# A decoder layer in fp32: operands of the second half of the tokens made one by one from sums kept in DRAM, its first weights split a pair ahead, and the zero blocks of attention written by ScalarE

## The chip, the cores and the metric

The kernel runs on one core of a Trainium2 chip. The metric is device time in microseconds (us), given as the median of three runs. All work is float32.

## The reference

One layer of a decoder with S = 2048 tokens, width D = 1024, 16 heads of 64 and an MLP of width 2752; cut to what matters:

```python
mod = silu(c) @ w_ada + b_ada              # shift, scale, gate for the mixer and for the MLP
h = rms_norm(x, g_attn) * (1 + scale_a) + shift_a
q_f, k_f, v_f, q_s, k_s, v_s, f_logit = split(h @ w_in)
o_fox = forgetting_attention(...)          # 8 heads: softmax(qk/8 + F[t] - F[s]), F = cumsum(log f)
o_sb = stick_breaking_attention(...)       # 8 heads: sigmoid(z) * prod of (1 - sigmoid(z)) between
mix = concat(head_rms_norm(o_fox), head_rms_norm(o_sb))
x = x + gate_a * (mix @ w_out)
h = rms_norm(x, g_mlp) * (1 + scale_m) + shift_m
u = causal_depthwise_conv(h @ w_up, conv_w, conv_b)   # w_up: 1024 x (2752 gate + 2752 value), width 3
x = x + gate_m * ((silu(u_gate) * u_val) @ w_down)
return rms_norm(x, g_final)
```

## The kernel before

*Split products.* A float32 factor is split into a high part (ScalarE copies it to the type fp32r) and a low part (VectorE or GpSimd subtracts the high part from it); `split`, lines 43 to 45, does both. A product is then three matmuls: high by high, high by low, low by high.

*Stages.* Projections and attention run first, interleaved unit by unit. In attention, blocks of weights are transposed on TensorE (L388) into a bank `ps_pt`, split into `at` (L392 on ScalarE, L393 on VectorE), and multiplied with V (L397). For a block on the causal diagonal the part of `at` ahead of the block is zero; `weighted` writes it at L391, 128 times in all, on GpSimd, which also multiplies the stick-breaking weights `a` (L420). Then the out-projection runs over eight units of 256 tokens (`mix` is its input, `x1` the residual). `finish_out` (L705) normalises a unit of `x1`, transposes it on TensorE, modulates it into `hf_m` (two buffers, ScalarE) and stores `hf_m` to DRAM (`hms`) from ScalarE's queue.

*Up-projection.* It runs over two halves of 1024 tokens (`sblk` 0 and 1), and in each over 21 pairs of 128 gate columns and 128 value columns, then over a tail of 64 and 64. A pair is a 2x2 by 2x2 block product (gate and value by two halves of D, two halves of D by two runs of 512 tokens), done with seven products for eight. Each product takes one of seven operands of the weights (`wu`, made anew for each pair from sums that GpSimd forms) and one of seven operands of h, numbered 0 to 6 (0, 2, 3 and 5 lie in `oa`, 1, 4 and 6 in `ob`), which serve a whole half. A product is four row blocks j of 128 by three matmuls of 512 columns: 12 matmuls, 84 a pair. The tail uses operands 0, 2, 3 and 5 alone: 48 matmuls.

`h_operands(sblk, j)` makes row j of all seven operands: two loads of 512 KB into `xh` on SyncE's (SP's) queue, four differences on GpSimd and VectorE, and the splits. Row 0 lies in the pool `hop0`, which is open from the out-projection on; rows 1 to 3 lie in `hop1`, opened over the space that the out-projection's pools held. Each row has one buffer, so the second half's row waits until the first half's last product has read it. The first pair of a half (`pair_first`, L821) goes row by row over seven banks:

```python
for j in range(NK):
    for s in (1, 4, 6, 0, 2, 5, 3):
        product(banks[s], ws[s], obs[j][0][s], j, j == 0, j == NK - 1)
```

In the other pairs (`pair`) each product runs whole, and the weight operands of the next pair (`nxt`) are made between its products. The weights of the first pair of each half are made beside `h_operands`.

*Down-projection.* `load` (L926) brings a block of `w_down` (`wdraw`, L935) and of the gated result (`graw`, L936) on SP's queue, and splits both; `xo` (L975) is the residual read back.

*Order.* Each engine and each queue works in order. The order is set by the framework's scheduler, which simulates the program and picks the next instruction for each engine; only dependencies, buffer counts and the order of the code steer it.

Of the kernel before, what the change touches and what calls it, by code (L numbers as in the profile page):

```python
# [16 lines left out]
P = 128  # L17
S = 2048
D = 1024
KT = D // P  # L20
# [13 lines left out]
def kernel(ctx: ExitStack, tc: tile.TileContext, x, c, w_ada, b_ada, g_attn, w_in, b_fgate,  # L34
# [17 lines left out]
    hms = [[dram.tile([P, 2 * TB], F32, name=f"hm{s}_{k}") for k in range(KT)] for s in range(2)]  # L52
# [329 lines left out]
    def weighted(o, kts, blk, V, hl, first, last, diag):  # L382
# [7 lines left out]
        if diag:  # L390
            nc.gpsimd.memset(f(at[:, :, 0:P]), 0.0)  # L391
# [313 lines left out]
    def finish_out(u, xts):  # L705
        sl = slice(u % 4 * HT, (u % 4 + 1) * HT)
# [3 lines left out]
        for kt in range(KT):  # L710
# [3 lines left out]
            hf = p2b.tile([P, HT], F32, name="hf_m", bufs=2)  # L714
            nc.scalar.activation(hf, ps[:, :HT], AF.Identity, scale=mod_m[:, 0, kt:kt + 1],
                                 bias=mod_m[:, 1, kt:kt + 1])
            nc.scalar.dma_start(hms[u // 4][kt][:, sl], hf)
# [21 lines left out]
    NK = KT // 2  # L739
    SB = 2 * TB  # L740
# [9 lines left out]
    def h_operands(sblk, j):  # L750

        pool = ho if j == 0 else ho1
        xh = ho.tile([P, 2, SB], F32, name="xh", bufs=2)
        for i in range(2):
            nc.sync.dma_start(xh[:, i], hms[sblk][j + i * NK])
        b = pool.tile([P, 3, 2, TB], F32R, name=f"ob{j}")
        a = pool.tile([P, 4, 2, TB], F32R, name=f"oa{j}")
        tt = ho.tile([P, 2, TB], F32, name="tt", bufs=1)
        t4 = wp.tile([P, TB], F32, name="t4", tag="ws", bufs=3)
        b11, b12 = xh[:, 0, 0:TB], xh[:, 0, TB:SB]  # L760
        b21, b22 = xh[:, 1, 0:TB], xh[:, 1, TB:SB]

        def put(hi, lo, s, lo_engine=None):
            split(hi, lo, s, lo_engine or nc.vector)

# [42 lines left out]
    def product(b, w, o, j, first, last):  # L808
        for i, (p, q) in enumerate(((0, 0), (0, 1), (1, 0))):
            nc.tensor.matmul(b, w[:, p, j], o[:, q], start=first and i == 0, stop=last and i == 2,  # L810
                             skip_group_check=True)

    def snap():
        return up_.tile([P, TB], F32, name="snap", bufs=4)
# [6 lines left out]
    def pair_first(ws, yg, yv):  # L821
# [3 lines left out]
        for j in range(NK):  # L825
            for s in (1, 4, 6, 0, 2, 5, 3):
# [194 lines left out]
```

## Time and profile before

| | |
|---|---|
| median of 3 runs | 3139.62 us (3137.22 to 3140.04) |
| the profiled execution | 3137.58 us, of it the profile's span 3135.8 |
| busy: TensorE matmuls, weight loads | 2962.9, 2508.4 us |
| busy: VectorE, ScalarE, GpSimd | 2142.5, 1650.2, 1281.3 us |
| DMA | 496.51 MB, mean 158 GB/s |
| projections and attention | to about 1590 us |
| out-projection | to 1776.2 us |
| up, first half, its first pair | to 2207.6 us, 1811.6 us |
| up, second half | to 2644.4 us |
| down | 2653.1 us to the end |

Times are from the span's start. A row of a group gives line, engine, operation, output, inputs, shape, count, then busy time and the mean of one in ns. A row of waits gives who waits, for whom, and us in all, times, longest. A row of the timeline gives start and length of a run of instructions, and in brackets the idle time ahead of it with what ended it. PE is TensorE, PEld its weight load, DVE VectorE, ACT ScalarE, POOL GpSimd, SPq the issuing of DMAs by SyncE.

### The profile page before, as it was taken

The numbers are of one execution on the slowest core, as the hardware profiler recorded it, in microseconds if no ns is written. First come the engines' busy times: TensorE is split into PE (matmuls) and PEld (weight loads), VectorE is DVE, ScalarE is ACT, GpSimd is POOL, SyncE is SP. The second block draws the span as 40 slices with busy tenths as digits, with TensorE's granted clock in tenths as the row PEclk, the third lists the DMA queues.
The fourth block names the chain that finished last, engine by engine and source line by source line (L and its number), as shares of the span: only waits on it lengthen the run. The fifth ranks groups of instructions, "written<-read, shape, count | busy, mean of one in ns | idle before, by whom it ended". The sixth has DMA issues, their size and how long they took to land. (4 is left out here: it accounts for less than half of the span.)

```text
span 3135.8 us, 46430 instructions
## 1 busy us (share of the span) xinstructions
PE 2962.9 (94%) x15934; PEld 2508.4 (80%) x15934; DVE 2142.5 (68%) x3334; ACT 1650.2 (53%) x3033; POOL 1281.3 (41%) x1523
## 2 busy tenths in 40 slices
PE   6889998999989999999999899999899998999998
PEld 5778787878878888888877688888678887888887
DVE  6787988888866765557832677778887776254253
ACT  5665666666656665567733444444444444333332
POOL 2564455456553343352212444444544442332321
PEclk8999999999999999999999999999999999999999
DMA  9447642556346796595456532223222223554552
GB/s 268 170 149 250 175 139 64 189 178 167 124 150 184 258 279 209 152 328 137 161 186 220 195 98 81 81 81 88 77 89 86 81 81 137 186 199 161 188 200 89
DMA packets 292940, 496.51 MB, mean 158 GB/s; under 512 B 29448, under 2 KB 177664, under 8 KB 291680
## 3 DMA queue, kind: packets, MB, share of 16 engines
q1 hardware_dynamic: 281072, 480.92, 48.0%
q10 hardware_dynamic: 11632, 12.63, 1.1%
q8 instruction: 126, 2.06, 0.3%
q14 instruction: 110, 0.90, 0.1%
HBM read 352.61 MB, written 90.51 MB: 141 GB/s over the span
## 5 line engine op out<-in xcount | busy, mean ns | idle before, releaser
L810 PE MATMUL ps_o<-oa,wu 128*128 128x512 f32 x2088 | 506.2, 393 | 18.1 <-DVE oa L45 12.0
L810 PEld LDWEIGHTS ps_o<-oa,wu 128*128 128x128 f32 x2088 | 392.4, 189 | 110.0 <-DVE oa L45 15.7
L397 PE MATMUL ps_pv<-at,V 128*128 128x256 f32 x2304 | 404.7, 294 | 36.2 <-DVE at L393 19.5
L393 DVE TENSOR_TENSOR at<-ps_pt,at 128x512 fp32r<-128x512 f32 (+1 forms) x576 | 364.0, 652 | 107.2 <-ACT at L392 104.2
L281 PE MATMUL ps_pj<-hp,w_qk 128*128 128x512 f32 x1512 | 415.2, 405 | 14.2 <-DMA hp<-hs 4.4
L392 ACT ACTIVATE at<-ps_pt 128x512 fp32r<-128x512 f32 (+1 forms) x576 | 314.4, 576 | 210.2 <-PE ps_pt L388 161.0
L420 POOL TENSOR_TENSOR a<-a,r 128x512 f32<-128x512 f32 (+3 forms) x240 | 286.8, 1196 | 309.8 <-DVE r L419 88.5
L397 PEld LDWEIGHTS ps_pv<-at,V 128*128 128x128 f32 x2304 | 334.6, 191 | 81.0 <-DVE at L393 34.5
L281 PEld LDWEIGHTS ps_pj<-hp,w_qk 128*128 128x128 f32 x1512 | 275.6, 191 | 68.7 <-DMA hp<-hs 6.9
L45 DVE TENSOR_TENSOR wd<-wdraw,wd 128x1024 fp32r<-128x1024 f32 x88 | 111.8, 1271 | 263.0 <-ACT wd L44 262.9
L45 POOL TENSOR_TENSOR g<-graw,g 128x512 fp32r<-128x512 f32 x84 | 142.3, 1696 | 326.5 <-ACT g L44 325.8
L378 PE MATMUL ps_qk<-K,Q 128*128 128x512 f32 (+2 forms) x640 | 265.7, 417 | 9.6 <-DMA K<-q 5.6
L419 DVE TENSOR_TENSOR_SCAN r<-r 128x513 f32<-128x513 f32 x192 | 258.9, 1360 | 19.4 <-ACT r L410 11.5
L960 PE MATMUL ps_o<-wd,g 128*128 128x512 f32 x1040 | 251.1, 391 | 8.7 <-ACT g L44 8.7
L810 PE MATMUL ps_t<-ob,wu 128*128 128x512 f32 x984 | 242.5, 391 | 0.3 <-ACT wu L44 0.3
L379 PE MATMUL ps_qk<-K,Q 128*128 128x512 f32 (+2 forms) x640 | 237.8, 373 | 0.0
L320 PE MATMUL ps_pj<-w_v,hp 128*128 128x256 f32 (+1 forms) x1536 | 230.8, 290 | 6.6 <-DVE q L290 2.9
L960 PEld LDWEIGHTS ps_o<-wd,g 128*128 128x128 f32 x1040 | 196.2, 189 | 50.0 <-ACT g L44 9.2
L44 ACT ACTIVATE wu<-wuraw 128x512 fp32r<-128x512 f32 x214 | 133.1, 626 | 184.2 <-PE ps_o L810 111.8
L320 PEld LDWEIGHTS ps_pj<-w_v,hp 128*128 128x128 f32 x1536 | 210.1, 193 | 16.5 <-DVE q L290 3.8
L810 PEld LDWEIGHTS ps_t<-ob,wu 128*128 128x128 f32 x984 | 185.3, 189 | 39.8 <-ACT wu L44 0.7
L44 ACT ACTIVATE wd<-wdraw 128x1024 fp32r<-128x1024 f32 x88 | 93.1, 1058 | 213.3 <-PE ps_bc L960 197.9
(218 smaller groups left out, 5834.1 us busy)
## 6 DMA issues: line engine op xcount, KB each, us to landing
hp<-hs SPq DMA_DIRECT2D x224, 512.0 KB
wuraw<-in_w_up_dram SPq DMA_DIRECT2D x84, 512.0 KB
wdraw<-in_w_down_dram SPq DMA_DIRECT2D x84, 512.0 KB
Q<-q SPq DMA_DIRECT2D x128, 256.0 KB
g<-u SPq DMA_DIRECT2D x42, 512.0 KB
graw<-g SPq DMA_DIRECT2D x84, 256.0 KB
hs<-hp SPq DMA_DIRECT2D x32, 512.0 KB
K<-q SPq DMA_DIRECT2D x128, 128.0 KB
```

Source lines behind the costliest of these rows:

```text
L45: (lo_engine or nc.gpsimd).tensor_sub(lo, src, f(hi))
L281: nc.tensor.matmul(acc, w[kt][:, a, n], h[:, bb], start=kt == 0 and i == 0, stop=kt == KT - 1 and i == 2)
L320: nc.tensor.matmul(av[:, t * width:(t + 1) * width], hts[kt][:, a, tok], w[1][kt][:, bb, 0:width], start=kt == 0 and m == 0, stop=kt == KT ...
L378: nc.tensor.matmul(b[:, :cw], Q[:, hl, 0, qcols], K[:, hl, :cw], start=True, stop=False)
L379: nc.tensor.matmul(b[:, :cw], Q[:, hl, 1, qcols], K[:, hl, :cw], start=False, stop=True)
L392: nc.scalar.activation(at[:, 0, lo:], b[:, lo:], AF.Copy)
L393: nc.vector.tensor_sub(at[:, 1, lo:], b[:, lo:], f(at[:, 0, lo:]))
L397: nc.tensor.matmul(o[:, 0:2 * P], V[kt // 4][:, kt % 4, hl, :], rhs, start=first and kk == 0 and w == 0, stop=last and kk == 1 and w == 1)
L419: nc.vector.tensor_tensor_scan(rev, rev, rev, 1.0, ALU.mult, ALU.bypass)
L420: (nc.vector if (ch + qi) % 4 == 0 else nc.gpsimd).tensor_mul(a[:, :need], a[:, :need], r[:, 1:need + 1])
L810: nc.tensor.matmul(b, w[:, p, j], o[:, q], start=first and i == 0, stop=last and i == 2, skip_group_check=True)
L960: nc.tensor.matmul(banks[t][n], g[:, a, t * P:(t + 1) * P], w[:, b, n * TB:(n + 1) * TB], start=k == 0 and i == 0, stop=k == NKD - 1 and i ...
```

## The change

The operands of h get one tile for each operand (`ob0` to `ob6`, all four rows in one tile, all in `hop1`) in place of one for each row. The normalised h goes to DRAM as quadrants (`hmo`, by half of D and run of 512 tokens), from four `hf_m` buffers. In the first half `h_rows(j)` makes row j of all seven with one split of 512 columns for each operand and row, 28 in all, every low part on VectorE. During the first half, after every third pair, `h_sums` loads a row of the second half's quadrants, forms the four sums on GpSimd and writes them back to DRAM. For the second half `h_operand(o)` loads one operand (1 MB) and splits it whole; its first pair goes operand by operand in the order 1, 4, 6, 0, 3, 2, 5. The weights of that pair are made during pair 20 of the first half. `wu` gets nine buffers for seven, `snap` three for four. In attention the zero block is a copy of zeros by ScalarE.

```diff
-            nc.gpsimd.memset(f(at[:, :, 0:P]), 0.0)
+            nc.scalar.activation(at[:, :, 0:P], edge[:, 0:2 * P].rearrange("p (a n) -> p a n", n=P), AF.Copy)
...
-            hf = p2b.tile([P, HT], F32, name="hf_m", bufs=2)
+            hf = p2b.tile([P, HT], F32, name="hf_m", bufs=4)
...
-            nc.scalar.dma_start(hms[u // 4][kt][:, sl], hf)
+            nc.scalar.dma_start(quadrants[kt // NK][:, kt % NK, sl], hf)
...
+    def square():
+        return ho.tile([P, 2, SB], F32, name="xh", bufs=2)
+
+    def h_quadrants(sblk, j):
+        x = square()
+        q = [x[:, i, n * TB:(n + 1) * TB] for i in range(2) for n in range(2)]
+        for part, o in zip(q, (0, B12, 2, 5)):
+            nc.sync.dma_start(part, hmo[sblk][o][:, j])
+        return q
+
+    def h_rows(j):
+
+        b11, b12, b21, b22 = h_quadrants(0, j)
...
         nc.gpsimd.tensor_sub(tt[:, 0], b22, b12)
         nc.gpsimd.tensor_sub(b12, b12, b11)
         nc.vector.tensor_sub(tt[:, 1], b22, b12)
         nc.vector.tensor_sub(t4, b21, tt[:, 1])
-        put(b[:, 0:2, 0], b[:, 0:2, 1], tt)
-        put(b[:, 2, 0], b[:, 2, 1], t4)
-        put(a[:, 0, 0], a[:, 0, 1], b11)
-        put(a[:, 1:3, 0], a[:, 1:3, 1], xh[:, 1].rearrange("p (a n) -> p a n", n=TB), nc.gpsimd)
-        put(a[:, 3, 0], a[:, 3, 1], b12)
-        return [a[:, 0], b[:, 1], a[:, 1], a[:, 3], b[:, 0], a[:, 2], b[:, 2]], a
+        for o, x in ((1, tt[:, 1]), (4, tt[:, 0]), (6, t4), (0, b11), (2, b21), (5, b22), (3, b12)):
+            split(obs[o][:, 0, j], obs[o][:, 1, j], x, nc.vector)
+
+    def h_sums():
+
+        for j in range(NK):
+            b11, b12, b21, b22 = h_quadrants(1, j)
+            nc.gpsimd.tensor_sub(b22, b22, b12)
+            nc.gpsimd.tensor_sub(b12, b12, b11)
+            nc.gpsimd.tensor_add(b11, b22, b11)
+            nc.gpsimd.tensor_sub(b21, b21, b11)
+            yield
+            for part, o in ((b22, 4), (b12, 3), (b11, 1), (b21, 6)):
+                nc.sync.dma_start(hmo[1][o][:, j], part)
+
+    def h_tile_of(o):
+        return ho1.tile([P, 2, NK, TB], F32R, name=f"ob{o}")
+
+    def h_operand(o):
+
+        raw = square().rearrange("p a (b n) -> p (a b) n", n=TB)
+        nc.sync.dma_start(raw, hmo[1][o])
+        b = h_tile_of(o)
+        split(b[:, 0], b[:, 1], raw, nc.vector)
+        return b
...
-        w = wp.tile([P, 2, NK, P], F32R, name="wu", bufs=7)
+        w = wp.tile([P, 2, NK, P], F32R, name="wu", bufs=9)
...
-        return up_.tile([P, TB], F32, name="snap", bufs=4)
+        return up_.tile([P, TB], F32, name="snap", bufs=3)
...
+        for j, s in ([(j, s) for j in range(NK) for s in ORDER] if by_row else
+                     [(j, s) for s in ORDER for j in range(NK)]):
+            product(banks[s], ws[s], obs[s], j, j == 0, j == NK - 1)
...
-            obs[j] = h_operands(sblk, j)
-            ws.extend(next(gen) for _ in range(2 if j < 3 else 1))
+        if sblk == 0:
+            for o in ORDER:
+                obs[o] = h_tile_of(o)
+            gen = w_operands(0)
+            ws = []
+            for j in range(NK):
+                h_rows(j)
+                ws.extend(next(gen) for _ in range(2 if j < 3 else 1))
+        else:
+            for o in ORDER:
+                obs[o] = h_operand(o)
+        sums = h_sums() if sblk == 0 else None
...
-            nxt = w_operands(ci + 1) if ci + 1 < NFULL else None
+            nxt = w_operands((ci + 1) % NFULL) if ci + 1 < NFULL or sblk == 0 else None
...
-            nc.sync.dma_start(gs[ci][sblk], ug)
+            stored = nc.sync.dma_start(gs[ci][sblk], ug)
+            if sums is not None and ci % 3 == 2:
+                with tc.issue_after(stored.ins):
+                    next(sums, None)
```

How the change moves instructions is shown at three places. The first is VectorE between the end of the out-projection and the first pair of the up-projection. Before (`x1` are the residual tiles, `ps_o` the out-projection's banks, `oa0` and `ob0` row 0 of the operands, `xh` its source):

```order
L45 TENSOR_TENSOR mix_21428<-o_21422,mix_21428 128x256
L633 TENSOR_TENSOR x1_21431<-ps_o_21459,x1_21431 128x512
L45 TENSOR_TENSOR oa0_21776<-xh_21772,oa0_21776 128x512
L633 TENSOR_TENSOR x1_21486<-ps_o_21488,x1_21486 128x512
L768 TENSOR_TENSOR tt_21777<-xh_21772 128x512
L45 TENSOR_TENSOR oa0_21776<-xh_21772,oa0_21776 128x512
L769 TENSOR_TENSOR t4_21778<-xh_21772,tt_21777 128x512
L45 TENSOR_TENSOR ob0_21775<-tt_21777,ob0_21775 128x2x512
L633 TENSOR_TENSOR x1_21486<-ps_o_21514,x1_21486 128x512
L45 TENSOR_TENSOR ob0_21775<-t4_21778,ob0_21775 128x512
```

The same place after (`ob1`, `ob4` and so on are now whole operands; the tiles `ss_m` hold the sums of squares of the normalisation):

```order
L636 TENSOR_TENSOR x1_21652<-ps_o_21654,x1_21652 128x512
L636 TENSOR_TENSOR x1_21652<-ps_o_21680,x1_21652 128x512
L98 RECIPROCAL ss_m_21707<-ss_m_21707 128x2
L713 TENSOR_SCALAR x1_21597<-x1_21597,ss_m_21707 128x1024
L713 TENSOR_SCALAR x1_21652<-x1_21652,ss_m_21707 128x1024
L45 TENSOR_TENSOR ob1_21772<-tt_21784,ob1_21772 128x512
L45 TENSOR_TENSOR ob4_21773<-tt_21784,ob4_21773 128x512
L45 TENSOR_TENSOR ob6_21774<-t4_21785,ob6_21774 128x512
L45 TENSOR_TENSOR ob0_21775<-xh_21779,ob0_21775 128x512
L45 TENSOR_TENSOR ob2_21777<-xh_21779,ob2_21777 128x512
```

The splits of row 0 stood between the last additions to the residual; now every split of the first half follows the normalisation of the last 256 tokens.

The second place is TensorE at the end of the first half. Before (numbers in 25000 belong to the second half's tiles, `ob0_24983` is its row 0; the others are the first half's):

```order
L810 MATMUL ps_o_24916<-oa3_21867,wu_24912 128x512 x3
L810 MATMUL ps_o_24917<-oa0_21776,wu_24912 128x512 x3
L810 MATMUL ps_o_24917<-oa1_21812,wu_24912 128x512 x3
L810 MATMUL ps_o_24917<-oa2_21840,wu_24912 128x512 x3
L810 MATMUL ps_o_24917<-oa3_21867,wu_24912 128x512 x3
L810 MATMUL ps_o_25098<-ob0_24983,wu_25013 128x512 x3
L810 MATMUL ps_t_25101<-ob0_24983,wu_25065 128x512 x3
```

After (names ending in 21772 to 21778 are the first half's operands, `ob4_25093` and `ob1_25088` the second half's):

```order
L830 MATMUL ps_t_24948<-ob4_21773,wu_24816 128x512 x9
L830 MATMUL ps_o_24896<-ob3_21776,wu_24799 128x512 x12
L830 MATMUL ps_t_25127<-ob4_25093,wu_24961 128x512
L830 MATMUL ps_o_24896<-ob5_21778,wu_24832 128x512 x12
L830 MATMUL ps_t_25127<-ob4_25093,wu_24961 128x512 x11
L830 MATMUL ps_o_25022<-ob0_21775,wu_25015 128x512 x2
L830 MATMUL ps_o_25023<-ob3_21776,wu_25015 128x512 x2
L830 MATMUL ps_o_25124<-ob1_25088,wu_24909 128x512 x9
L830 MATMUL ps_t_24948<-ob6_21774,wu_24848 128x512 x12
```

The second half's first products, of operands 4 and 1, now stand among the first half's last, ahead of the tail.

The third place is SP's queue between the up-projection and the down-projection. Before (`u` holds the gated result, `g21_1` its tail in DRAM):

```order
L952 DMA gm_28155<-gate_m_234 128x1024
L953 DMA gf_28156<-in_g_final_dram 128x1024
L935 DMA wdraw_28168<-in_w_down_dram 128x1024
L936 DMA graw_28169<-g0_0_140 128x512
L935 DMA wdraw_28202<-in_w_down_dram 128x1024
L936 DMA graw_28203<-g1_0_142 128x512
L935 DMA wdraw_28236<-in_w_down_dram 128x1024
L975 DMA xo_28821<-x1s0_192 128x1024
L975 DMA xo_28864<-x1s1_193 128x1024
L975 DMA xo_28907<-x1s2_194 128x1024
L975 DMA xo_28950<-x1s3_195 128x1024
L923 DMA g21_1_183<-u_28141 64x1024
```

After:

```order
L984 DMA gf_28182<-in_g_final_dram 128x1024
L1006 DMA xo_28847<-x1s0_192 128x1024
L1006 DMA xo_28890<-x1s1_193 128x1024
L1006 DMA xo_28933<-x1s2_194 128x1024
L1006 DMA xo_28976<-x1s3_195 128x1024
L954 DMA g21_1_183<-u_28167 64x1024
L966 DMA wdraw_28194<-in_w_down_dram 128x1024
L967 DMA graw_28195<-g0_0_140 128x512
L966 DMA wdraw_28228<-in_w_down_dram 128x1024
```

The first loads of `w_down` stood ahead of the residual's loads and of the store of the tail; now they stand behind both.

More of the change, by code (lines that the diff above doesn't have):

```diff
@@ L51 @@
     os_ = [[dram.tile([P, TB], F32, name=f"os{p}_{t}") for t in range(NTB)] for p in range(NPAIR)]
[L52 removed]
+    NK = KT // 2
+    SB = 2 * TB
+    B12 = 7
+    hmo = [[dram.tile([P, NK, TB], F32, name=f"hm{s}_{o}") for o in range(8)] for s in range(2)]
     gs = [[dram.tile([P if k < NFULL else REST, 2 * TB], F32, name=f"g{k}_{s}") for s in range(2)]
@@ L809, in product @@
         for i, (p, q) in enumerate(((0, 0), (0, 1), (1, 0))):
-            nc.tensor.matmul(b, w[:, p, j], o[:, q], start=first and i == 0, stop=last and i == 2,
+            nc.tensor.matmul(b, w[:, p, j], o[:, q, j], start=first and i == 0, stop=last and i == 2,
                              skip_group_check=True)
     def snap():
-        return up_.tile([P, TB], F32, name="snap", bufs=4)
+        return up_.tile([P, TB], F32, name="snap", bufs=3)
     def y_tile():
@@ L842, in run @@
             for j in range(NK):
-                product(b, ws[s], obs[j][0][s], j, first and j == 0, j == NK - 1)
+                product(b, ws[s], obs[s], j, first and j == 0, j == NK - 1)
             if nxt is not None:
@@ L905 @@
         a, b = bank_a(), bank_a()
-        oa = [obs[j][1] for j in range(NK)]
         for j in range(NK):
-            product(a, w1, oa[j][:, 0], j, j == 0, j == NK - 1)
+            product(a, w1, obs[0], j, j == 0, j == NK - 1)
         p1 = snap()
```

33 lines of the change are left out of this document (8 added, 25 removed).

## The prediction

> **What bounds the kernel now.** I read the page's first part and its slices first, to see which engine is full and where it is not; then a table of stretches around the three change-overs of the second half; then the waits of TensorE in each of them, and the timeline at their edges.
>
> ```profile
> PE 2962.9 (94%) x15934; PEld 2508.4 (80%) x15934; DVE 2142.5 (68%) x3334; ACT 1650.2 (53%) x3033; POOL 1281.3 (41%) x1523
> PE   6889998999989999999999899999899998999998
> ```
>
> TensorE (PE) is the bound: 2962.9 of 3135.8 us. A change that leaves its matmuls alone can only win what it idles or runs slowly. The 8s in slices 23, 29 and 34 are the three change-overs around the halves of the up-projection, the last 8 is the program's end. The stretches, with columns of busy time and count for PE, PEld, DVE, ACT and POOL, then granted clock, DMA share and GB/s:
>
> ```profile
> 1776.20:1811.60 35.40, 27.22 (x106) 19.77 (x105) 28.03 (x25) 20.29 (x35) 23.03 (x13) 0.86 0.43 147
> 1811.60:2207.60 396.00, 394.58 (x1729) 323.25 (x1728) 315.71 (x358) 179.38 (x253) 168.38 (x168) 1.00 0.27 82
> 2200.00:2262.00 62.00, 48.94 (x182) 36.48 (x181) 58.51 (x55) 30.81 (x42) 33.65 (x19) 0.89 0.24 72
> 2641.00:2655.00 14.00, 5.27 (x20) 3.95 (x20) 8.36 (x8) 5.76 (x7) 1.81 (x1) 0.79 0.76 269
> 2180.94 2.88 PE L810 MATMUL ps_t<-ob,wu 128*128 128x512 f32 x12
> 2183.66 5.60 PE L810 MATMUL ps_o<-oa,wu 128*128 128x512 f32 x24
> ```
>
> The last two rows give the pitch of a matmul at full clock: 12 from 2180.94 to 2183.66, 0.227 us each. At the middle change-over, 182 matmuls are worth 41.3 us, so the stretch 2200 to 2262 loses 20.7 us. VectorE (DVE) is busy 58.51 of those 62 us: it makes the operands. Inside the first half (1811.6 to 2207.6) PE idles 1.4 us. The waits of TensorE (us, times, longest) in the out-projection, the middle and the down change-over, and of ScalarE (ACT) in the out-projection:
>
> ```profile
> PE ps_t L713 <- ACT hf_m L715: 8.2, 9, 1.8
> PE ps_o L629 <- ACT mix L44: 2.8, 4, 1.0
> ACT hf_m L715 <- DMA hm<-hf_m: 8.6, 6, 3.8
> ACT mix L44 <- DMA hm<-hf_m: 8.1, 3, 2.7
> PE ps_o L810 <- DVE oa L45: 8.9, 4, 4.2
> PE ps_o L960 <- ACT g L44: 8.7, 1, 8.7
> ```
>
> **The change, part by part.**
>
> *Middle change-over: a gain of 17 us.* Today no product of the second half starts before the row of operands it needs is split, and the rows of `oa` stay occupied until the first half's last product. By the order, the new operands 4 and 1 are used while the first half's tail still runs, and the weights are there. What stays is the splitting on DVE:
>
> ```profile
> L45 DVE TENSOR_TENSOR oa<-xh,oa 128x512 fp32r<-128x512 f32 x8 | 13.3, 1688 | 0.0
> L45 DVE TENSOR_TENSOR ob<-tt,ob 128x1024 fp32r<-128x1024 f32 x4 | 4.9, 1218 | 0.4 <-ACT ob L44 0.4
> L45 POOL TENSOR_TENSOR oa<-xh,oa 128x1024 fp32r<-128x1024 f32 x4 | 13.6, 3411 | 0.0
> L45 DVE TENSOR_TENSOR wu<-wuraw,wu 128x512 fp32r<-128x512 f32 x8 | 5.3, 682 | 0.7 <-ACT wu L44 0.7
> ```
>
> Seven splits of 128x2048 are an estimated 2.3 us each on DVE (twice the 1218 ns of 1024 columns, less a start), 16 us in all, and 2 us each on ACT. A 512-column split costs 682 ns alone and 1688 ns beside GpSimd's (POOL's) 3411 ns splits, which go. An operand feeds 12 matmuls, 2.7 us, so 2.3 us keeps up if DVE has little else. It has: at 315.71 of 396 us it is 80% full, so in the 45 us from the pair before to the end of the first pair some 9 us are free for 16; the deeper weight buffers carry part of the rest. Bounds: the whole 20.7 us goes, or, if DVE binds as now, none. I take 4 us left, near the first end, because the splits now spread over the pair before: 17 gained.
>
> *Out-projection: a gain of 7 us.* Four `hf_m` buffers for two. ACT waited 8.6 and 8.1 us for their stores, in front of `hf_m` and `mix`; PE waited 8.2 and 2.8 us behind those. Bounds 0 and 11.0; I take 7, since the bank waits in the 8.2 also include ACT's own work.
>
> *First change-over: a loss of 6.5 us.* By the order, the 28 splits of 512 columns now all follow the normalisation of the last tokens on DVE, and on ACT the last `hf_m`, where before row 0's stood earlier and products started at once:
>
> ```profile
> 1774.48 1.87 PE L629 MATMUL ps_o<-wo,mix 128*128 128x512 f32 x7
> 1776.18 0.85 PE L810 MATMUL ps_o<-ob,wu 128*128 128x512 f32 x3
> 1811.58 2.88 PE L810 MATMUL ps_o<-oa,wu 128*128 128x512 f32 x12
> 1787.82 1.40 DVE L709 TENSOR_SCALAR x<-x,ss_m 128x1024 f32<-128x1024 f32 x2
> 1780.94 1.04 ACT L93 ACTIVATE junk_m<-x 128x1024 bf16<-128x1024 f32 x1
> 1791.34 1.00 ACT L715 ACTIVATE hf_m<-ps_t,mod_m 128x256 f32<-128x256 f32 x2
> 1794.69 1.00 ACT L715 ACTIVATE hf_m<-ps_t,mod_m 128x256 f32<-128x256 f32 x2
> L766 POOL TENSOR_TENSOR tt<-xh 128x512 f32<-128x512 f32 x3 | 5.0, 1675 | 12.0 <-DVE ob L45 12.0
> ```
>
> Call the end of the out-projection T0 (1776.2); the first pair ends at 1811.6, T0+35.4. After: an add, a square, root, reciprocal and two products, about 4 us (1.04 and 1.40 are the large ones); then four pairs of `hf_m`, 1.0 us each with their issues, 3.35 us apart at 1791.34 and 1794.69 with two buffers; I take 2.1 apart with four, 8.5 us. So the first split stands at T0+12.5. Then 28 splits and 6 sums at 0.64 us (682 ns, starts overlapping a little) are 21.8 us; six POOL differences of 1675 ns each slow one DVE step by 1.0 (1688 less 682), 6 us; the last products 1.6. End at T0+41.9, 6.5 later. Bounds: nothing, if the splits find POOL quiet and `hf_m` runs through, to 28 us, if all 28 cost 1688 ns.
>
> *Sums through DRAM: 0.* Sixteen POOL steps of 1675 ns, 16 loads and 16 stores of 256 KB, 7 loads of 1 MB, SP's queue with them. Cover: DVE has 80 us free in the first half and DMA stands at 0.27. If that cover were gone, 16 DVE steps lose 1.0 us each, 16 us; below nothing, the 1.4 us that PE idles, since two more weight buffers are there. Nearer to zero, as 16 is a fifth of the free 80. One `snap` buffer fewer: covered by the same slack; each is read within a pair.
>
> *Down change-over: a loss of 6 us.* The chain there, and what SP's queue issues:
>
> ```profile
> 2636.75 7.64 PE L810 MATMUL ps_o<-oa,wu 128*128 128x512 f32 x33
> 2653.12 2.07 PE L960 MATMUL ps_o<-wd,g 128*128 128x512 f32 x4 [8.73 <-ACT g L44]
> 2645.30 0.44 SPq L935 DMA_DIRECT2D wdraw<-in_w_down_dram  x1
> 2648.05 3.76 SPq L975 DMA_DIRECT2D xo<-x1s  x4
> 2652.44 0.48 SPq L923 DMA_DIRECT2D g<-u  x1
> 2651.49 1.06 ACT L44 ACTIVATE wd<-wdraw 128x1024 fp32r<-128x1024 f32 x1 [1.26 <-DMA wdraw<-in_w_down_dram]
> ```
>
> The first `wdraw` is issued at 2645.30, lands at 2651.5, and PE goes on at 2653.12. In the new order four `xo` loads and the store of the tail's result (2652.44 now, after its convolution, SiLU and product) stand ahead of it in SP's in-order queue. So it is issued near 2652.9, 7.6 us later; the landing, 6.2 us, may be shorter as the 2 MB of `xo` go first. Bounds 0 (if the tail is stored sooner) and 9; I take 6.
>
> *Zero blocks: 0.* 128 of them move from POOL to ACT:
>
> ```profile
> L391 POOL MEMSET at<- x128: 301/312/318, 51.1 to 1583.8; 128x256 f32 x128
> L44 ACT ACTIVATE mix<-o 128x256 fp32r<-128x256 f32 x56 | 23.1, 416 | 71.4 <-POOL o L614 62.8 <-DMA hm<-hf_m 8.1 <-ACT hf_m L715 0.4
> POOL at L391 <- PE ps_pv L397: 160.4, 54, 18.2
> ACT at L392 <- PE ps_pt L388: 161.0, 153, 5.9
> PE ps_pv L397 <- ACT at L392: 4.8, 6, 1.6
> PE ps_pt L388 <- POOL a L420: 10.8, 14, 1.9
> ```
>
> ACT's nearest row has 416 ns, 53 us for 128: the upper bound, all on the path. POOL waits 160.4 us with a zero block at the head of its queue and the products `a` behind it; PE waited 10.8 us for those: the gain at best. ACT mostly waits for the transposes at this place (161.0 us) and hides the zeros there, while PE waited only 4.8 us on ACT. I take 0 between, and the stage is ordered anew, so it holds most of my uncertainty.
>
> Sum: -17 - 7 + 6.5 + 0 + 6 + 0 = -11.5 us. The profiled execution took 3137.58 us (span 3135.8 and 1.8 around it): 3126.1. The median of the runs shown, 3139.62, is 2.0 higher, so on its scale 3128.
>
> **Two rules beside the rows.** After the 8.73 us of idling, the first four matmuls took 2.07 us, more than twice the 0.227 pitch. The Trainium skill, "TensorE: Matmul & The Clock Gate", section "What's actually happening", says that an idle window of about 3.4 us halves the clock until some 3.4 us of work have passed; the row agrees. It speaks against this change: the new idling after T0 would start the first pair at half clock. By the rule that adds up to 1.7 us, an estimate from the page's window; by the rows nothing, since the splits pace those products, and I keep nothing.
>
> A DVE split took 1688 ns beside POOL's against 682. The skill's "SBUF — State Buffer", section "Who interferes with whom", says that a VectorE step with two SBUF inputs contends with a GpSimd step that reads SBUF, not with one that only writes. The slowing agrees; by the rule the removed zero blocks free no VectorE time, which the sum has as 0 already, and the sixteen sums would each block it whole, an estimated 27 us for my 16, still inside the 80 free.
>
> **The rivals.**
> 1. *DVE keeps the middle bound* (0.16). For it: 58.51 of 62 us busy and 16 us of splits that remain. Against it: POOL's 3411 ns splits are gone and the work starts earlier. Then 4 gained for 17: 1.5 us slower, 3141.
> 2. *The first change-over eats the gain; slower* (0.12). All seven tiles lie where out-projection weights and residual tiles lay. If POOL keeps DVE at 1688 ns for all 28 splits, the loss is 28 for 6.5: 10 us slower, 3150. It decides slower from a loss of 24 us on. Against it: only six POOL differences stand there.
> 3. *ACT becomes the bound in attention* (0.09). If half of the 53 us is on the path: 15 us slower, 3155. For it: 1650.2 us busy grows by 53. Against: the 161.0 us.
> 4. *POOL freed pays as well* (0.13). The 10.8 us of PE waits go: 3117.
>
> **How the numbers follow.** My own forecast has 0.50, about 3121 to 3136 from the bounds near each value taken. A change of less than 0.2%, 6.3 us, can't be told from none here: 3133.3 to 3145.9. Faster: 0.43 of the forecast's 0.50 and rival 4's 0.13, 0.56. Same: 0.07 and rival 1's 0.16, 0.23. Slower: rivals 2 and 3, 0.21. The range 3112 to 3150 reaches to rivals 4, 1 and 2 and leaves out 3 and the far ends.
>
> **What the profile after would show.** Right, if PE runs through the middle with under 6 us of waits, restarts 13 to 16 us after the last up product at the down change-over, and stands still some 12 us after the out-projection before its first product. Wrong, if DVE is full again between the halves with PE waiting on its splits, if the splits after the out-projection average over a microsecond, or if PE's waits in attention move by more than 10 us in sum.

## The result and the profile after

The changed kernel takes 3177.47 us (median of 4 runs, 3171.45 to 3181.12) where the kernel before takes 3139.83 (4 runs): a ratio of 1.0112, 95% interval 1.0099 to 1.0125. It is slower by 1.1%; the forecast was 0.4% faster. The profiled execution has a span of 3173.4 us for 3135.8, 37.6 us more. The page's first part and TensorE's slices:

```profile
PE 2974.2 (94%) x15934; PEld 2515.6 (79%) x15934; DVE 2115.2 (67%) x3329; ACT 1683.9 (53%) x3156; POOL 1196.0 (38%) x1395
PE   6889998989989999999999899999999998999998
```

The 8 of the middle change-over (slice 29) is gone, as meant. The engines' sums hardly differ; the loss is spread. To find it, the up-projection's matmuls were counted over the trace: a stretch that ends with the same number of them has about the same work in both kernels. The stretches run from the out-projection's end to matmul 168 (the first two pairs), from 252 to 1680 (first half), from 1680 to 2064 (middle), from 2064 to 3624 (second half). First the four of before, then the four of after; columns are length, then busy time and count of PE, PEld, DVE, ACT and POOL (the counts take in what straddles an edge, and at the start the last transposes), granted clock, DMA share, GB/s:

```profile
1776.20:1831.00 54.80, 46.40 (x189) 35.33 (x187) 45.93 (x45) 29.74 (x48) 33.08 (x24) 0.91 0.35 114
1850.70:2177.30 326.60, 326.10 (x1431) 267.45 (x1430) 255.38 (x290) 144.43 (x205) 138.04 (x136) 1.00 0.27 83
2177.30:2288.50 111.20, 95.72 (x384) 74.29 (x383) 99.03 (x100) 51.27 (x71) 57.00 (x40) 0.94 0.29 88
2288.50:2646.00 357.50, 355.60 (x1562) 291.97 (x1560) 273.21 (x314) 156.42 (x219) 145.94 (x105) 1.00 0.26 79
...
1782.80:1846.40 63.60, 51.23 (x189) 37.47 (x188) 49.78 (x62) 33.70 (x58) 22.71 (x21) 0.84 0.29 91
1866.00:2219.10 353.10, 334.10 (x1428) 269.47 (x1429) 255.78 (x292) 143.98 (x207) 141.68 (x152) 0.99 0.36 105
2219.10:2315.80 96.70, 90.45 (x386) 73.62 (x386) 78.72 (x84) 50.20 (x60) 38.50 (x29) 0.96 0.44 132
2315.80:2678.00 362.20, 356.09 (x1561) 291.91 (x1559) 258.16 (x312) 152.66 (x216) 121.30 (x105) 1.00 0.26 78
```

The end of attention is marked by its last sums over heads (`headsel`), first in the kernel before, then after:

```profile
1588.94 0.61 PE L485 MATMUL ps_pt<-headsel,sq 128*128 128x2 f32 x4 [1.68 <-POOL sq L480]
1602.05 0.61 PE L488 MATMUL ps_pt<-headsel,sq 128*128 128x2 f32 x4 [1.68 <-POOL sq L483]
```

| stretch | forecast, us | measured, us |
|---|---|---|
| projections and attention (zero blocks) | 0 | +13.1 |
| out-projection (187.3 before, 180.8 after) | -7 | -6.5 |
| first change-over, two pairs | +6.5 | +8.8 |
| first half | 0 | +26.5 |
| middle change-over | -17 | -14.5 |
| second half | 0 | +4.7 |
| down change-over (from matmul 3624 to the restart: 7.1, 14.1) | +6 | +7.0 |
| the rest | 0 | -1.5 |
| sum | -11.5 | +37.6 |

The edges of the rows lie up to 1.7 us beside the matmul that they stand for. Taken at the matmuls themselves, the first half lost 25.8 us, the middle gained 14.9, the second half lost 5.3 and the down change-over 6.6 (TensorE idles 15.30 us there for 8.73), so terms and differences of such rows are good to a microsecond or two.

Four terms came out within 2.5 us. The three that had been costed at nothing brought 44 us. Where the four show, in the changed kernel's timeline of TensorE and the queue of SP:

```profile
1781.32 1.63 PE L632 MATMUL ps_o<-wo,mix 128*128 128x512 f32 x6
1794.58 0.79 PE L830 MATMUL ps_o<-ob,wu 128*128 128x512 f32 x1 [1.88 <-ACT ob L44]
2239.45 0.80 PE L830 MATMUL ps_t<-ob,wu 128*128 128x512 f32 x1 [5.32 <-ACT ob L44]
2692.13 2.07 PE L991 MATMUL ps_o<-wd,g 128*128 128x512 f32 x4 [15.30 <-ACT g L44]
...
2677.55 2.32 SPq L1006 DMA_DIRECT2D xo<-x1s  x4
2683.95 0.48 SPq L954 DMA_DIRECT2D g<-u  x1
2684.53 0.53 SPq L966 DMA_DIRECT2D wdraw<-in_w_down_dram  x1
```

No product for 11.6 us after the out-projection; one wait of 5.32 us left in the middle; and at the down change-over 15.30 us of idling, with the first weights issued behind the residual and the tail's store.

### The profile page after: what moved, and what is told of

It reads as the page before. It is cut to its first block, busy times and chain, and to the rows that moved or that the text cites. A ratio compares the mean times of both kernels' runs of the same rounds, so it can differ in the third digit from the quotient of the medians.

```text
span 3173.4 us, 46552 instructions
## 1 busy us (share of the span) xinstructions
PE 2974.2 (94%) x15934; PEld 2515.6 (79%) x15934; DVE 2115.2 (67%) x3329; ACT 1683.9 (53%) x3156; POOL 1196.0 (38%) x1395
## 5 line engine op out<-in xcount | busy, mean ns | idle before, releaser
L830 PE MATMUL ps_o<-ob,wu 128*128 128x512 f32 x2592 | 631.6, 396 | 32.7 <-DVE snap L881 16.0
L830 PEld LDWEIGHTS ps_o<-ob,wu 128*128 128x128 f32 x2592 | 490.7, 191 | 151.5 <-DVE snap L881 23.0
L830 PE MATMUL ps_t<-ob,wu 128*128 128x512 f32 x1008 | 253.5, 391 | 5.3 <-ACT ob L44 5.3
L391 PE MATMUL ps_pt<-edge,a 128*128 128x128 f32 x1088 | 187.1, 280 | 28.1 <-POOL a L423 14.3
```

The source lines that it names most:

```text
L830: nc.tensor.matmul(b, w[:, p, j], o[:, q, j], start=first and i == 0, stop=last and i == 2, skip_group_check=True)
```

## What holds up the first half

After every third pair four sums run on GpSimd. One such place in the changed kernel, POOL, then DVE, then PE:

```profile
1962.52 1.96 POOL L778 TENSOR_TENSOR xh<-xh 128x512 f32<-128x512 f32 x1 [5.20 <-DMA xh<-hm]
1964.44 1.74 POOL L822 TENSOR_TENSOR wuraw<-wuraw,ws 128x512 f32<-128x512 f32 x1
1966.14 2.27 POOL L779 TENSOR_TENSOR xh<-xh 128x512 f32<-128x512 f32 x1
1968.49 1.61 POOL L780 TENSOR_TENSOR xh<-xh 128x512 f32<-128x512 f32 x1
1970.18 2.13 POOL L781 TENSOR_TENSOR xh<-xh 128x512 f32<-128x512 f32 x1
...
1963.23 1.80 DVE L45 TENSOR_TENSOR wu<-wuraw,wu 128x512 fp32r<-128x512 f32 x1
1964.95 2.31 DVE L900 SCALAR_TENSOR_TENSOR u<-y,conv,u 128x1024 f32<-128x1024 f32 x1
1967.18 1.78 DVE L45 TENSOR_TENSOR wu<-ws,wu 128x512 fp32r<-128x512 f32 x1
1968.88 2.30 DVE L901 SCALAR_TENSOR_TENSOR u<-y,conv,u 128x1024 f32<-128x1024 f32 x1
1971.11 1.75 DVE L45 TENSOR_TENSOR wu<-wuraw,wu 128x512 fp32r<-128x512 f32 x1
1973.92 0.68 DVE L881 TENSOR_TENSOR snap<-ps_o,snap 128x512 f32<-128x512 f32 x1
1974.65 4.61 PE L830 MATMUL ps_o<-ob,wu 128*128 128x512 f32 x12 [4.20 <-DVE snap L881]
```

For 9.8 us GpSimd runs with no gap, and five VectorE steps of 0.68 or 1.28 us take 1.75 to 2.31. Each loses about 1.07 us, 5.3 in all. The step that reads a product's bank (L881) comes late and TensorE stands 4.20 us; the 12 matmuls behind take 4.61 us, where the prediction's row of 12 had 2.88. The Trainium skill, "SBUF — State Buffer", section "Who interferes with whom", has a VectorE step with two SBUF inputs contend with GpSimd's reads. The five steps agree.

## The experiments

All ratios are against the kernel before on the same chip, in five rounds, with 95% intervals.

**The zero blocks alone.**

```diff
-            nc.gpsimd.memset(f(at[:, :, 0:P]), 0.0)
+            nc.scalar.activation(at[:, :, 0:P], edge[:, 0:2 * P].rearrange("p (a n) -> p a n", n=P), AF.Copy)
```

> The kernel before, with only the zero blocks moved from GpSimd to ScalarE. In the changed kernel the last matmul of attention stands 13.1 us later than before (1602.05 for 1588.94). Theory: ScalarE's 128 zero copies are on the path there, so this edit alone gives about 13 us: 3153 for 3140. Rival: the 13 us come from elsewhere (the attention stage was ordered anew by the whole change, or runs differ): within 4 us of 3140.

Measured 1.0034 [1.0021, 1.0047], 10.7 us. In its profile attention ends at 1604.10, 15.2 us later. Its zero blocks and TensorE's waits; the last row is of the kernel before:

```profile
L391 ACT ACTIVATE at<-edge 128x256 fp32r<-128x256 f32 x128 | 53.3, 417 | 19.4 <-PE ps_pv L397 18.8
PE ps_pv L397 <- DVE at L393: 23.3, 34, 1.3
PE ps_pt L388 <- POOL a L420: 14.2, 19, 1.9
PE ps_pv L397 <- ACT at L392: 8.6, 8, 4.5
...
PE ps_pv L397 <- DVE at L393: 19.5, 32, 1.5
```

The 53.3 us of copies stand ahead of the copies of the transposes on ScalarE, VectorE's second half of the split follows those, and TensorE waits for both. Its waits for GpSimd's products rose from 10.8 to 14.2: GpSimd was freed and nothing came of it.

**The zero blocks put back in the changed kernel**, and the changed kernel again.

```diff
-            nc.scalar.activation(at[:, :, 0:P], edge[:, 0:2 * P].rearrange("p (a n) -> p a n", n=P), AF.Copy)
+            nc.gpsimd.memset(f(at[:, :, 0:P]), 0.0)
```

> The changed kernel with the zero blocks back on GpSimd, all else kept. Theory of the copies on the path: attention ends 13 us earlier, 3164 for 3177. Rival: the order, not the copies: within 5 us of 3177.

> The changed kernel itself once more, beside the three that follow, so that they are compared on one chip. With the zero blocks back on GpSimd it stood at 1.0125 of the kernel before, measured on another chip than the changed kernel's 1.0112. If ScalarE's copies cost in the changed kernel what they cost alone (10.7 us), the changed kernel stands above that, near 1.016; if the rest of the change hides them, at 1.011 to 1.013.

Measured 1.0125 [1.0109, 1.0141] with the blocks put back, and 1.0119 [1.0103, 1.0134] for the changed kernel again. Attention ended at 1592.47 and at 1604.13, so 11.7 us were won there; in the whole nothing shows, and intervals of 0.0016, some 5 us, on either side would hide a gain of a few us. This was tried once more below.

**The sums on VectorE.**

```diff
-            nc.gpsimd.tensor_sub(b22, b22, b12)
+            nc.vector.tensor_sub(b22, b22, b12)
...
```

> The changed kernel with the sixteen sums of the second half's operands formed by VectorE in place of GpSimd; loads, stores and places stay. In the first half TensorE now loses 26 us more between its 252nd and 1680th matmul than before. Theory: GpSimd's sums hold VectorE's steps at half speed (0.68 us becomes 1.8) and stand in front of GpSimd's weight sums; then most of the 26 us goes: about 3155. Rival: it is SyncE's queue and the transfers (eight issues ahead of each weight load): within 6 us of 3177. Second rival: VectorE has no room for the 11 us of sums: 3180 or more.

Measured 1.0081 [1.0069, 1.0093], some 12 us better than 1.0119: between the theory (3155) and the first rival (within 6 us). On VectorE the sums cost less, but they are not free there.

**The sums left out, and the traffic too.**

```diff
-            nc.gpsimd.tensor_sub(b22, b22, b12)
...
             yield
```

> The changed kernel with the sixteen sums left out; the loads and stores around them stay, so the second half multiplies by unsummed quadrants. With the sums on VectorE the first half lost 21.0 us between its 252nd and 1680th matmul, on GpSimd 29.4, before the change 3.0. Theory A: what is left is the sums' own time on an engine that the weight operands need: the loss falls under 8 us, about 21 us less than the changed kernel. Theory B: it is SyncE's queue, eight issues and a wait ahead of the next weight load: the loss stays at 15 us or more.

```diff
-        nc.sync.dma_start(raw, hmo[1][o])
+        nc.sync.dma_start(raw, hmo[1][{1: 0, 3: B12, 4: 5, 6: 2}.get(o, o)])
...
-        sums = h_sums() if sblk == 0 else None
+        sums = None
```

> The changed kernel without the sums and without their loads and stores; the second half's operands are loaded from the unsummed quadrants. Theories A and B both expect the first half's loss at 3 to 6 us, 24 us less than the changed kernel in all. Rival: nine wu buffers, three snap buffers and the new order of the half are to blame: the loss stays above 12 us.

Measured 1.0069 [1.0057, 1.0082] and 1.0067 [1.0053, 1.0080]. No cost of the loads and stores shows; the sums' time costs 1.0119 less 1.0069, about 16 us. The first half (matmul 252 to 1680) in the changed kernel again, with sums on VectorE, without sums, without sums and traffic, and with sums spread (below):

```profile
1868.00:2224.20 356.20, 337.27 (x1428) 272.44 (x1429) 256.66 (x291) 143.66 (x206) 142.62 (x152) 0.97 0.36 104
1870.00:2214.80 344.80, 331.37 (x1427) 268.30 (x1428) 247.41 (x308) 143.08 (x207) 109.02 (x136) 0.99 0.37 107
1868.00:2206.00 338.00, 329.37 (x1428) 268.11 (x1429) 239.08 (x290) 142.99 (x206) 114.14 (x136) 0.99 0.37 109
1866.00:2204.40 338.40, 327.92 (x1429) 267.01 (x1429) 239.56 (x291) 143.43 (x207) 112.12 (x138) 1.00 0.27 79
1860.00:2204.90 344.90, 330.34 (x1428) 267.79 (x1429) 245.34 (x292) 143.45 (x207) 139.46 (x154) 1.00 0.37 108
```

VectorE's busy time falls from 256.66 to 239.08 us with the same number of steps: 17.6 us of contention. But without sums the stretch is 338.0 us, still 11.4 above the 326.6 of before. Something else holds the halves.

**The sums spread, one a pair.**

```diff
+            yield
             nc.gpsimd.tensor_sub(b22, b22, b12)
+            yield
...
-            if sums is not None and ci % 3 == 2:
-                with tc.issue_after(stored.ins):
+            if sums is not None and ci >= 1:
+                with tc.issue_after(stored.ins), tc.issue_after(halos[0].ins):
```

> The changed kernel with GpSimd's sixteen sums spread, one a pair from the second pair on, in place of four in a row after every third pair; loads and stores as before. The sums' time cost 16 us (1.0119 with them, 1.0069 without). Theory: it is the burst, some 9 us in which VectorE goes at half speed and the weight sums stand behind; one sum a pair fits in VectorE's room of 5 us a pair, so nearly all of the 16 us goes: 1.007 to 1.008. Rival: each sum costs TensorE its own microsecond wherever it stands: within 0.15% of the changed kernel's 1.0119.

Measured 1.0081 [1.0067, 1.0095], 12 of the 16 us. VectorE's busy time fell by 11.3 us too: spread, the sums meet fewer steps that they slow. So most of the cost is the burst's; how much of that is VectorE's slowing, and how much GpSimd's weight sums that stand behind the four, was not separated.

**Buffers.** In the changed kernel the numbers of `wu` and `snap` buffers are nine and three; before they were seven and four.

```diff
-        w = wp.tile([P, 2, NK, P], F32R, name="wu", bufs=9)
+        w = wp.tile([P, 2, NK, P], F32R, name="wu", bufs=8)
...
-        return up_.tile([P, TB], F32, name="snap", bufs=3)
+        return up_.tile([P, TB], F32, name="snap", bufs=4)
```

> The changed kernel with four snap buffers as before, and eight wu buffers for nine to make room. ScalarE waits 53 us in the first half and 44 us in the second for a snap buffer, in 13 and 15 times. Theory: this wait delays the banks and TensorE behind them: about 8 us in the first half and 5 in the second, 3164. Rival: the wait lies beside other work: 3172 to 3182.

With 7 for 8 and 4 snap buffers:

> The changed kernel with seven wu and four snap buffers, as before the change. Without any sums the two halves still lost 14.7 and 10.5 us (between their 252nd and 1680th matmul, and from the 252nd on) where before they lost 3.0 and 3.8, with ScalarE waiting 53 and 54 us for a snap buffer and TensorE behind it on the steps that read snap. Theory: the third snap buffer binds; both halves lose 8 to 12 us less, 1.006. Rival: the order of the weights a pair ahead needs nine buffers, or the order itself is worse: no gain, or slower as with eight and four (1.0152).

With nine and four, where `tt` shares a buffer of `u` to make room:

> The changed kernel with nine wu and four snap buffers; the room comes from tt, which takes a u buffer. With seven and four the second half fell to its loss of before (3.4 us), but the middle change-over lost 16 us for 9.5; with eight and four the second half lost 20. Theory: the third snap buffer is what both halves lose by, and nine wu buffers keep the middle: the second half loses 4 us, the first 8 less than the changed kernel, 1.0119 becomes about 1.008. Rival: any count of wu other than seven shifts the weights against the products and costs the halves, so with nine and four the second half still loses over 8 us.

With seven and three:

> The changed kernel with seven wu buffers and still three snap buffers. The second half lost (from its 252nd matmul on) 3.4 us with seven wu and four snap buffers, 8.6 with nine and three, 21.2 with eight and four, 11.2 with nine and four. Theory: the count of wu buffers sets it, since with more than seven the weights' splits are queued ahead and ScalarE stands for them with the convolutions behind it; so seven and three lose 3 to 5 us. Rival: the third snap buffer costs by itself: 8 us or more.

Measured, in that order: 1.0152 [1.0139, 1.0165], 1.0092 [1.0078, 1.0106], 1.0137 [1.0118, 1.0157], 1.0143 [1.0126, 1.0161]. The second half (matmul 2064 to 3624) with eight and four, seven and four, nine and four, seven and three:

```profile
2317.10:2692.00 374.90, 358.29 (x1562) 291.49 (x1560) 266.73 (x312) 149.93 (x215) 124.79 (x104) 1.00 0.28 83
2318.90:2676.00 357.10, 355.30 (x1561) 291.92 (x1560) 274.07 (x314) 154.79 (x216) 143.37 (x105) 1.00 0.27 79
2325.10:2690.00 364.90, 358.12 (x1561) 291.46 (x1560) 255.81 (x310) 151.01 (x215) 120.46 (x104) 1.00 0.28 85
2323.80:2690.00 366.20, 358.82 (x1562) 291.44 (x1560) 281.06 (x313) 155.27 (x218) 145.21 (x105) 1.00 0.28 85
```

Only seven and four reach the 357.5 of before (357.1). Nine and three have 362.2; one snap buffer fewer costs 9.1 at seven, and one `wu` buffer more costs 17.8 at four. At nine the snap buffers make no such difference (362.2 with three, 364.9 with four, the latter with `tt` moved). So both numbers hold the half, and together. None of the four theories came as a whole: with eight and four the time came out above theory and rival; with seven and four the second half came back, but the middle took 103.3 us for the changed kernel's 95.8 in the run of 1.0119; with nine and four, and with seven and three, it was the rival that came. What stands in the way with nine and four, ACT and PE:

```profile
2429.90 0.63 ACT L44 ACTIVATE wu<-ws 128x512 fp32r<-128x512 f32 x1 [8.77 <-POOL ws L818]
2430.43 1.23 ACT L898 ACTIVATE u<-y,conv 128x1024 f32<-128x1024 f32 x1
2443.07 3.04 PE L830 MATMUL ps_o<-ob,wu 128*128 128x512 f32 x12 [0.36 <-DVE snap L881]
```

ScalarE stands 8.77 us with a split of the next pair's weights at its queue's head, whose source GpSimd has not formed yet; the convolution waits behind it, VectorE gets its work late, and the step that frees a bank is 0.36 us late. TensorE's waits from 2320 to 2640 us with seven and four, eight and four, nine and four, seven and three:

```profile
PE ps_o L830 <- DVE snap L881: 0.8, 1, 0.8
PE ps_o L830 <- DVE snap L881: 11.3, 9, 1.7
PE ps_o L830 <- DVE snap L881: 2.5, 7, 0.6
PE ps_o L830 <- ACT wu L44: 3.7, 7, 0.6
```

With all gaps counted, TensorE idles there 1.1, 13.5, 5.1 and 7.1 us, in the changed kernel 4.9 and before 0.3; all but those 3.7 us are ended by VectorE's steps on the banks (L877 and L881). The lengths of the half, taken at the matmuls, rank in the same order, from 355.8 before to 374.2 with eight and four. What makes these steps late is argued only: from 2320 to 2640 us ScalarE waited so for 86.5 us with seven and four, 115.0 with eight and four, 135.9 with nine and four. With three snap buffers this wait is 83.7 (seven) and 88.5 (nine), but 41.3 and 47.2 us of waiting for a snap buffer come beside it. So wherever one of the two waits stands above that of seven and four the half is longer; but ScalarE's wait is longest with nine and four and the half is longest with eight and four, so how the one becomes the other was not settled.

The run with nine and four also lost at the first change-over, from the move of `tt`: its first product came 26.8 us after the out-projection for 11.6, of which 11 to 12 us were still there at matmul 168. TensorE idled 16.81 us behind a weight split, since GpSimd formed the first weight sums only at 1801.20, behind the sums into `tt`; in the changed kernel they were formed at 1759.37, during the out-projection.

**The zero blocks again**, beside the run with nine and four:

> The kernel with nine wu and four snap buffers and the zero blocks back on GpSimd, to settle the zero blocks on one chip. Alone, the copies on ScalarE cost 1.0034 of the kernel before; put back in the changed kernel they gained nothing that showed between two chips. Theory: they cost attention 10 us in either kernel: 0.3% under the run beside it. Rival: within 0.1% of it.

Measured 1.0125 [1.0107, 1.0143] for 1.0137. Attention ended 6.6 us earlier (1592.88 for 1599.46); at the end of all the medians are 0.9 us apart. So the copies delay attention in every pair of runs (15.2, 11.7 and 6.6 us), and cost 10.7 us in the kernel before. Over all profiled executions attention ended at 1594.2 to 1604.3 in the twelve with copies on ScalarE and at 1586.5 to 1593.4 in the six with zeros from GpSimd: the two never overlap, but the size varies from one execution to the next. With nine and four, the 6.6 us went again in the up-projection, which the edit does not touch; why the changed kernel does not keep what it wins is open.

**The down change-over.**

```diff
+        w = dp.tile([P, 2, D], F32R, name="wd", bufs=6)
         wraw = dp.tile([P, D], F32, name="wdraw", bufs=3)
         graw = dp.tile([P, TB], F32, name="graw", bufs=2)
-        w = dp.tile([P, 2, D], F32R, name="wd", bufs=6)
...
-            nc.sync.dma_start(xt, x1s[row])
+            with tc.issue_after(loaded_g[2]) if tb == 0 else ExitStack():
+                nc.sync.dma_start(xt, x1s[row])
...
-        nc.sync.dma_start(gs[NFULL][sblk], sg[REST:P])
+        (nc.gpsimd if sblk else nc.sync).dma_start(gs[NFULL][sblk], sg[REST:P])
```

> The changed kernel with the down-projection's first weight loads ahead in SyncE's queue: their buffers lie where xh lay, the residual's loads are queued behind the third block, and the last two stores of the gated result go through GpSimd's queue. TensorE idled 15.3 us at the down change-over in the changed kernel (8.7 before the change). Theory: SyncE's queue is the whole of it; TensorE idles 7 us or less, and the time falls by about 8 us. Rival: the tail's convolution on ScalarE and VectorE, which stands ahead of the first split, sets the restart: a gain of 2 us at most.

Measured 1.0097 [1.0083, 1.0111], 7 us less. The first `wdraw` is issued 15.8 us before TensorE's idling begins (at 2685.55), where in the changed kernel it came 7.7 us after (2676.83), and the idling is halved:

```profile
2669.73 0.48 SPq L968 DMA_DIRECT2D wdraw<-in_w_down_dram  x1
2693.04 2.07 PE L994 MATMUL ps_o<-wd,g 128*128 128x512 f32 x4 [7.49 <-ACT g L44]
```

The 7.49 that are left fit the rival, by which the tail's steps stand ahead of the first split on ScalarE; no run took them away.

**Everything mended.** The first attempt carried the move of `tt`:

> The changed kernel mended in all places found so far: zero blocks on GpSimd, sums spread one a pair, four snap buffers, the first weights of the down-projection ahead in SyncE's queue (gm and gf behind them too). If the terms add (sums 12, snap 8, down 8, zero blocks 8 to 10), 36 us come off the changed kernel's 37 of loss: 1.000, within 0.2%. Rival: they overlap, and it stays at 1.004 or more.

Measured 1.0069 [1.0055, 1.0083]: its rival. TensorE idled 16.81 us behind the weight split here too, and the second half took 363.7 us between its matmuls, where before it took 355.8. The second, with seven and four:

> The changed kernel mended once more with seven wu and four snap buffers as before the change, tt left where it was (moved to a u buffer, it delayed the first product of the up-projection by some 18 us), zero blocks on GpSimd, sums spread, first weights of the down-projection ahead. From the 1.0092 with seven and four buffers alone: spread sums 12 us less, down change-over 7, zero blocks 5 to 10: 1.000 to 1.002. Rival: the spread sums cost more where only seven wu buffers stand ahead: 1.004 or more.

Measured 1.0001 [0.9992, 1.0009]: the terms account for the loss. Beside the changed kernel in the run of 1.0119, attention ends 10.8 us earlier, and between the same matmuls the first half is 20.3 us shorter, the second half 7.4, the down change-over 6.1. In its profile the first half and the second (matmul 252 to 1680, and from 2064 on; the middle lies between the two rows):

```profile
1862.40:2198.00 335.60, 328.18 (x1430) 268.05 (x1429) 253.84 (x287) 143.19 (x202) 155.52 (x152) 0.99 0.36 107
2292.90:2650.00 357.10, 355.73 (x1561) 291.99 (x1560) 273.66 (x314) 154.57 (x216) 142.22 (x105) 1.00 0.28 84
```

The middle takes 2292.9 less 2198.0, 94.9 us for 111.2, so the idea is worth 16.3 us. It pays 9.0 in the first half, where the sums are formed (spread, with nine and three buffers, they cost some 5 of it; the rest was not traced), and 7.4 from attention's end (1593.37) to the first product (1788.02), which before had the operands of row 0. Together these leave nothing. Beside the run with spread sums and nine and three buffers, the first half is 7.7 us shorter (335.7 for 343.4 between the matmuls): the buffers' part of it.

**The kernel before, mended.**

```diff
-            hf = p2b.tile([P, HT], F32, name="hf_m", bufs=2)
+            hf = p2b.tile([P, HT], F32, name="hf_m", bufs=3)
...
+            with tc.issue_after(loaded_g[2]):
+                nc.sync.dma_start(gm, gate_m)
...
```

> The kernel before with two edits that worked: three hf_m buffers for two (there is no room for four), and the first loads of the down-projection ahead of gm, gf, the residual and the last two stores in SyncE's queue. The out-projection gave 6.4 us with four buffers, so 4 with three; of the 8.7 us at the down change-over 4 may go, since ScalarE's split stands behind the tail's steps. 0.9975. Rival: the order elsewhere shifts and eats it: 0.999 to 1.002.

Measured 0.9985 [0.9975, 0.9996]: 0.15% under the kernel before, between theory and rival. `wdraw` is issued 16.3 us before the up-projection's end (2645.13), and TensorE idles 3.57 us for 8.73, then 0.90 more:

```profile
2628.88 0.37 SPq L937 DMA_DIRECT2D wdraw<-in_w_down_dram  x1
2648.70 1.20 PE L960 MATMUL ps_o<-wd,g 128*128 128x512 f32 x4 [3.57 <-ACT g L44]
```

The out-projection showed no gain from the third `hf_m` buffer: from attention's end to the first product 188.8 us for 187.2.

## Why the prediction was wrong

*Middle change-over: right.* 14.5 us gained for 17 forecast, with one wait of 5.3 us left for the 4 allowed.

*Out-projection: right in size, with some luck.* 6.5 us for 7. The waits that it went by fell as meant, ScalarE's for DMAs from 16.7 to 4.4 us, but TensorE's behind them only from 11.0 to 7.6, half of what was gained. That three buffers gave nothing in the kernel before leaves open whether the number of buffers, the new place of the stores, or the splits of row 0, which no longer stand between the last additions, did the rest.

*First change-over: right.* 8.8 us lost for 6.5. VectorE's splits ran from 11.6 to 43.7 us after the out-projection, for 12.5 to 40.3 as worked out, at 0.89 us each. What the sum had kept at nothing is the clock: the granted clock is 0.84 for 0.91 in this stretch, and TensorE is busy 51.23 us for 46.40 with the same matmuls.

*Down change-over: right, to a microsecond.* 7.0 for 6, by the queue as forecast: with the loads ahead, the wait falls from 15.30 to 7.49 us.

*Sums through DRAM: the step that failed.* The price was there (16 us, "if that cover were gone"), and 16 us is what the sums' time cost. The step took zero, the value near the other end, because VectorE has 80 us free over the half. But the sums come four together, and in those 9.8 us VectorE is full and falls 5.3 us behind, against a room of 4.2 us a pair (326.6 less 255.4 us, over 17 pairs), with GpSimd's weight sums behind them as well. Spread one a pair, the same sums cost 4 us. An average over the half was used for a burst.

*One snap buffer fewer and two weight buffers more: costed at nothing, or as a small gain.* "Each is read within a pair" was true and did not decide it. Changed one at a time they cost 9.1 and 17.8 us in the second half, and together about 5 there and 7.7 in the first (beside the same spread sums). The order on ScalarE's and VectorE's queues is made anew by the scheduler for each number of buffers, and was not read there.

*Zero blocks: costed at nothing; the mechanism is that of the rival on ScalarE, at half its price or less.* 10.7 us alone, 13.1 in the stretch, between the 0 that was taken and the 26.5 of the rival, which had half of the 53 us on the path (its 15 is the time of the whole change). The argument that ScalarE mostly waits at this place (161 us) failed: TensorE's waits for ScalarE and for the VectorE steps behind it rose all the same. A mean of idle time says nothing about the moment when a diagonal block comes.

The first rival (VectorE keeps the middle) did not come: VectorE is busy 78.72 of 96.70 us there. Nor did the second: the splits averaged 0.89 us, not 1.69, and 8.8 us were lost, not 28. The fourth (GpSimd freed pays) fell: TensorE's waits for GpSimd's products rose (10.8 to 14.2 with the copies alone).

## What to carry to other kernels

Compare a new load with the room in the stretch where it lands, one pair long, not with the average over a stage: the same sixteen sums cost 16 us in bursts of four and 4 us one by one. A larger buffer count is a change of order, not only of room: check what then stands at the head of each in-order queue, and what it waits for. And where a transfer lands late, read what its queue holds ahead of it: taking the residual's loads and the last stores out from there gave 7 us in the changed kernel and, with a third `hf_m` buffer that showed no gain of its own, took 0.15% off the kernel before.

## What the runs showed that was not expected

A VectorE step of 128x512 from two SBUF tiles takes 1.75 to 1.80 us for 0.68 beside GpSimd's sums, and VectorE's busy time over the half grows by 17.6 us for sixteen sums, 1.1 us each. Sixteen loads and sixteen stores of 256 KB beside the up-projection show no cost (1.0069 with, 1.0067 without, each to 0.0013). After 4.20 us of idling, 12 matmuls took 4.61 us for 2.88, so that stall was worth 5.9 us; after 2.45 us they took 3.06. The granted clock was 0.68 from 1974.6 to 1980 and 1.00 from 2038 to 2042. The Trainium skill, "TensorE: Matmul & The Clock Gate", section "What's actually happening", has the clock halved after an idle window of about 3.4 us, which runs free; these two agree. A third differs: after 3.19 us of idling, less than that window, 12 matmuls took 5.49 us and the granted clock was 0.50 from 2109.3 to 2115.0; here the trace decides.

```profile
2038.04 3.06 PE L830 MATMUL ps_o<-ob,wu 128*128 128x512 f32 x12 [2.45 <-DVE snap L881]
2109.30 5.49 PE L830 MATMUL ps_o<-ob,wu 128*128 128x512 f32 x12 [3.19 <-DVE snap L877]
```
